# A mixture-of-experts stage: router weights applied on leaving PSUM, one-pass combine products, one-hot matrices built a pair ahead, and nine weight granules allowed ahead

## The chip, the core and the metric

The kernel runs on one core of a Trainium2 chip. The core has a matmul engine (PE, with its weight loads listed apart as PEld), a vector engine (DVE), a scalar engine (ACT), GpSimd (POOL) and a sync engine (SP), which here only issues DMAs. Matmul results land in PSUM, in eight banks of 128 x 512 float32; everything else lives in SBUF. The metric is the device time of one execution in microseconds (us), as the median of several runs. The profiled execution has its own time, and the rows shown are from it.

## The reference, cut to what matters

Two transformer-like blocks follow each other on 256 tokens of width 1024. The change touches the first block's mixture of experts alone: each token picks one of four groups and two of the eight experts in it, so 32 experts see on average 16 tokens each. All arithmetic is float32.

```python
def hier_moe(xn, w_gr, b_gr, w_er, b_er, w_gate, w_up, w_down):
    ...
    top_v, top_i = lax.top_k(e_logits, TOP_K_IN_GROUP)
    wts = g_prob[:, None] * jax.nn.softmax(top_v, axis=-1)
    ...
    def expert_block(args):
        tok_b, e = args
        xb = xpad[tok_b]
        h = jax.nn.silu(xb @ w_gate[e]) * (xb @ w_up[e])
        return h @ w_down[e]
    out = lax.map(expert_block, (buf_tok.reshape(n_blk, MOE_BLOCK), blk_expert))
    out = out.reshape(rows, d) * buf_wt[:, None].astype(out.dtype)
    y = jnp.zeros((t + 1, d), out.dtype).at[buf_tok].add(out)[:t]
```

## The kernel before, in words

The program goes through the first block's mixers (span 0 to about 130 us), the router (to about 148 us), the mixture of experts (148 to 625 us), the second block's attention (to about 810 us) and its table lookups (to the end). Every engine executes its instructions in the order in which the program issues them; waits are semaphores that the framework places by tile.

**Slots.** Each expert has 64 slots (a branch, `overflow`, serves inputs in which an expert gets more, and is passed over here). `Pp` holds, for each token and expert, the token's slot (1 to 64, or 0), `Wt` its router weight. For a group of four experts `Dm` (L749) is the 0/1 matrix tokens x slots, made on DVE by comparing `Pp` with a row of numbers. `gather(g)` (L747) multiplies the normalised tokens by it: 32 matmuls at L762, whose results leave PSUM through ACT and DVE into `xg`. `Dw` (L753) is the same matrix times `Wt`, made on POOL.

**Pairs.** The loop at L791 takes 16 pairs of experts; pair p uses group p // 2. For each pair PE does, in this order: the gate products (L807, two experts side by side in the array's columns), the combine of the pair before, the up products (L807 again), two transposes of `Dw` (L817), four of the hidden activations `hs` (L823), in an odd pair the gather of the next group, and the down products (L842). The combine (L775) multiplies `dT`, the transposed weighted matrix, by the experts' outputs `eo`: four float32 matmuls of 128 x 512, each of which the profile counts as two instructions; DVE adds each result to the residual `res` (L777). `dT`, `hT` and the two halves of `eo` leave PSUM by `evac` (L119), which alternates between ACT and DVE, so `dT` and the first half of `eo` go by ACT and `hT` and the second half of `eo` by DVE.

**Weight granules.** Each expert has three weight matrices of 128 x 4096 float32, 2 MiB each; one such load is called a granule here. A pair takes six, the stage 96 (numbered here 0 to 95), all issued by SP at L309 in the order of use. `pump` (L299) emits loads, `free` says that a granule was used. Until granule 45 the granules go around nine buffers, six of `ring` and three of `ring2` (L644); then, since `ring2` is closed before pair 8 (L793), around six. `pump` emits a load when no more than `cap` = 6 granules are emitted and not freed. On the chip a load starts when the last reader of its buffer's former granule is done.

**The end of the stage.** In pair 15 the combine is split: its first half stands among the last down products (L840), the second at the end (L847). Behind each of its four results DVE multiplies by the final gain (L784) and ACT takes two sums of squares (L144), which the next stage's scaling waits for. ACT also splits the first chunks of the next stage's weights there (L164).

Of the kernel before, what the change touches and what calls it, by code (L numbers as in the profile page):

```python
# [8 lines left out]
F32 = mybir.dt.float32  # L9
F32R = mybir.dt.float32r  # L10
# [21 lines left out]
NRING = 6  # L32
NRING2 = 3
# [31 lines left out]
def _body(tc, A, out, dbg):  # L65
    nc = tc.nc
# [10 lines left out]
    with ExitStack() as ctx:  # L77
# [219 lines left out]
        R2_END = n_pre + 5 * (NRING + NRING2)  # L297

        def pump():  # L299
            while st["emitted"] < len(src) and st["emitted"] < st["freed"] + st["cap"]:  # L300
                i = st["emitted"]
                if rg[1] is None and n_pre + NRING <= i < n_pre + NRING + NRING2:
                    break
                p = rg[1] if rg[1] is not None and n_pre <= i < R2_END and (i - n_pre) % (NRING + NRING2) >= NRING else rg[0]
                w = p.tile([128, 4096], F32, tag="w", name="w")
                n = src[i].shape[1]
                for o in range(0, n, 1024 if i == 0 else n):
                    v = slice(o, o + (1024 if i == 0 else n))
# [338 lines left out]
        if True:  # L647
# [70 lines left out]
            with pool("p2b", 2) as q, pool("p2c", 1) as q1:  # L718
# [5 lines left out]
                def weights():  # L724

                    gd = pq.tile([128, 2, 4], F32, name="gd")
                    nc.vector.tensor_tensor(gd, gl, gm[:, :, None].to_broadcast([128, 2, 4]), op=ALU.subtract)
                    ge = pq.tile([128, 2, 4], F32, name="ge")
                    nc.scalar.activation(ge, gd, AF.Exp)
                    pe = pq.tile([128, 2, 2], F32, name="pe")  # L730
                    nc.vector.tensor_tensor(pe, tv[:, :, 0:2], tv[:, :, 0:1].to_broadcast([128, 2, 2]), op=ALU.subtract)
                    nc.scalar.activation(pe, pe, AF.Exp)
                    preload(AF.Silu)
                    gs = pq.tile([128, 2], F32, name="gs")
                    nc.vector.tensor_reduce(gs, ge, axis=AX.X, op=ALU.add)
                    s2 = pq.tile([128, 2], F32, name="s2")
                    nc.vector.tensor_reduce(s2, pe, axis=AX.X, op=ALU.add)
                    nc.vector.tensor_tensor(s2, s2, gs, op=ALU.mult)
                    nc.vector.reciprocal(s2, s2)
                    nc.vector.tensor_tensor(pe, pe, s2[:, :, None].to_broadcast([128, 2, 2]), op=ALU.mult)  # L740
                    nc.vector.tensor_tensor(E2, E2, pe[:, :, :, None].to_broadcast([128, 2, 2, 32]), op=ALU.mult)
                    nc.vector.tensor_tensor(Wt, E2[:, :, 0], E2[:, :, 1], op=ALU.add)
                    mc = pq.tile([128, 1], F32, name="mc")
                    nc.vector.tensor_reduce(mc, b2[:, 0:32], axis=AX.X, op=ALU.max)
                    nc.vector.tensor_copy(most, mc)

                def gather(g):  # L747
                    Dm = q1.tile([128, 2, 4, 64], F32R, name="Dm")
                    nc.vector.tensor_tensor(Dm, Pp[:, :, 4 * g:4 * g + 4, None].to_broadcast([128, 2, 4, 64]), io64, op=ALU.is_equal)  # L749
                    if g == 0:  # L750
                        weights()
                    Dw = q1.tile([128, 2, 4, 64], F32, name="Dw")
                    nc.gpsimd.tensor_tensor(Dw, Dm.bitcast(F32), Wt[:, :, 4 * g:4 * g + 4, None].to_broadcast([128, 2, 4, 64]), op=ALU.mult)  # L753
                    xg = q.tile([128, 8, 4, 64], F32, name="xg")
                    for kk in range(4):
                        b = bank()
                        for j in range(2):
                            k = 2 * kk + j
                            i = 0
                            for tt in range(2):  # L760
                                for hl in range(2):
                                    nc.tensor.matmul(b[:, j * 256:(j + 1) * 256], xh[:, hl, tt, k * 128:(k + 1) * 128],  # L762
                                                     Dm[:, tt].rearrange("p e s -> p (e s)"), start=(i == 0), stop=(i == 3))
                                    i += 1
                        for j in range(2):
                            k = 2 * kk + j
                            evac(xg[:, k].rearrange("p e s -> p (e s)"), b[:, j * 256:(j + 1) * 256], gc[:, C_N2 + k:C_N2 + k + 1], eng="av"[kk % 2])
                    G[g] = (xg, Dw)

                def combine(pend, then=None, halves=(0, 1)):  # L770
                    dT, eo = pend
                    for half in halves:
                        for tt in range(2):
                            b = bank()
                            nc.tensor.matmul(b, dT[:, tt * 128:(tt + 1) * 128], eo[:, half * 512:(half + 1) * 512], start=True, stop=True)  # L775
                            rs = res[:, tt, half * 512:(half + 1) * 512]
                            nc.vector.tensor_tensor(rs, rs, b, op=ALU.add)  # L777
                            if then is not None:
                                then(tt, half)


                def both(tt, half):
# [2 lines left out]
                    quarter_sq(res, ss, hs, tt, half, "a")  # L785
                    quarter_sq(yy, ss2, hs, tt, half, "a")

                gather(0)
                pend = None
                pyx = ExitStack()  # L790
                for p in range(16):  # L791
# [6 lines left out]
                        yy = py.tile([128, 2, D], F32, name="yy")  # L798
                        ss2 = py.tile([128, 2, 2], F32, name="ss2")
                    g, pr = p // 2, p % 2  # L800
                    xg, Dw = G[g]
                    pg, pu = bank(), bank()
                    for dst in (pg, pu):
                        w = [get(), get()]
# [4 lines left out]
                        free(2)  # L809
                        if dst is pg and pend is not None:  # L810
                            combine(pend)
                    hs = q.tile([128, 512], F32, name="hs")
                    nc.scalar.activation(hs, pg, AF.Silu)
                    nc.vector.tensor_tensor(hs, hs, pu, op=ALU.mult)  # L814
                    b = bank()
                    for tt in range(2):
                        nc.tensor.transpose(b[:, tt * 128:(tt + 1) * 128],  # L817
                                            Dw[:, tt, 2 * pr:2 * pr + 2].rearrange("p e s -> p (e s)"), ident)
                    dT = q1.tile([128, T], F32, name="dT")
                    evac(dT, b[:, :T])  # L820
                    b = bank()
                    for f in range(4):
                        nc.tensor.transpose(b[:, f * 128:(f + 1) * 128], hs[:, f * 128:(f + 1) * 128], ident)  # L823
# [2 lines left out]
                    if pr == 1 and g < 7:  # L826
                        gather(g + 1)
                    w = [get(), get()]
                    eo = q1.tile([128, D], F32, name="eo")
                    bh = [bank(), bank()]  # L830
                    pend = (dT, eo)
                    for half in range(2):
# [5 lines left out]
                        for f in range(4):  # L838
                            if p == 15 and half and f == 2:
                                combine(pend, both, (0,))  # L840
                            for j in range(2):
                                nc.tensor.matmul(bh[half][64 * j:64 * j + 64, :], hT[:, f, 64 * j:64 * j + 64],  # L842
                                                 w[j][:, f * 1024 + half * 512:f * 1024 + half * 512 + 512],
                                                 start=(f == 0), stop=(f == 3))
                        evac(eo[:, half * 512:(half + 1) * 512], bh[half])
                    free(2)
                combine(pend, both, (1,))  # L847
            dump("h2", res)
# [613 lines left out]
```

## Time and profile before

| what | us |
|---|---|
| median of 3 runs (1549.41 to 1551.52) | 1549.61 |
| the profiled execution | 1549.71 |
| its span, first to last instruction | 1547.9 |
| PE busy over the span | 1330.8 (86%) |
| DVE busy | 774.8 (50%) |
| POOL busy | 399.4 (26%) |
| ACT busy | 383.9 (25%) |

The program moves 530 MB, 343 GB/s over the span. A span's average says little here: the stages have different limits, so the rows below are of the mixture of experts alone. "issue" in the chain of waits is time in which an engine waited for nothing that the profile shows. The granted clock is the share of the full TensorE clock that was granted in a stretch.

### The profile page before, as it was taken

The numbers are of one execution on the slowest core, as the hardware profiler recorded it, in microseconds if no ns is written. First come the engines' busy times: TensorE is split into PE (matmuls) and PEld (weight loads), VectorE is DVE, ScalarE is ACT, GpSimd is POOL, SyncE is SP. The second block draws the span as 40 slices with busy tenths as digits, with TensorE's granted clock in tenths as the row PEclk, the third lists the DMA queues.
The fourth block names the chain that finished last, engine by engine and source line by source line (L and its number), as shares of the span: only waits on it lengthen the run. The fifth ranks groups of instructions, "written<-read, shape, count | busy, mean of one in ns | idle before, by whom it ended". The sixth has DMA issues, their size and how long they took to land.

```text
span 1547.9 us, 16059 instructions
## 1 busy us (share of the span) xinstructions
PE 1330.8 (86%) x5543; PEld 712.6 (46%) x5543; DVE 774.8 (50%) x1796; ACT 383.9 (25%) x873; POOL 399.4 (26%) x355
## 2 busy tenths in 40 slices
PE   9899999999999999999999757877788777877777
PEld 7776334343344343788878723332333333332332
DVE  4756122122112121667577998877644544544453
ACT  6634000000000001546645322222111111111111
POOL 1211000000000000243111324444544445544441
PEclk9999999999999999999999878999998899999899
DMA  9526899996999999744330669999999999999994
GB/s 390 211 109 272 344 426 426 429 426 283 419 412 429 425 415 429 281 177 150 112 134 15 252 269 420 420 419 420 420 421 419 421 420 420 419 420 420 420 420 168
DMA packets 57748, 530.21 MB, mean 343 GB/s; under 512 B 6593, under 2 KB 6849, under 8 KB 9409
## 3 DMA queue, kind: packets, MB, share of 16 engines
q0 software_dynamic: 37936, 272.65, 42.8%
q1 hardware_dynamic: 19440, 256.35, 40.0%
q8 instruction: 46, 0.75, 0.2%
q14 instruction: 38, 0.30, 0.1%
q10 hardware_dynamic: 288, 0.16, 0.0%
HBM read 528.08 MB, written 1.05 MB: 342 GB/s over the span
## 4 chain that ended last, share of the span: by engine, by line
PE 27%; DMA 26%; DVE 8%; issue 8%; POOL 5%; ACT 1%; POOLq 0%; DVEq 0%; ACTq 0%
DMA rw<-in_uv_dram,ei 26%; PE b L807 7%; PE b L234 6%; POOL rw L1245 4%; PE b L842 4%; PE acc L1266 2%; DVE jk L1250 2%; PE b L775 2%; PE b L263 1%; PE b L247 1%; PE b L762 1%; DVE sl L165 1%; PE b L1014 1%; DVE i L1211 1%; DVE i L1216 0%
## 5 line engine op out<-in xcount | busy, mean ns | idle before, releaser
L1266 PE MATMUL acc<-rw,dg 128*128 128x512 f32 x1024 | 501.5, 648 | 148.6 <-ACT dg L1263 148.6
L1250 DVE SCALAR_TENSOR_TENSOR jk<-rw,xr 128x1024 f32<-128x1024 f32 x256 | 313.7, 1226 | 245.4 <-DMA rw<-in_uv_dram,ei 245.2
L1266 PEld LDWEIGHTS acc<-rw,dg 128*128 128x128 f32 x1024 | 206.9, 207 | 443.2 <-issue 233.3
L1245 POOL DMA_INDIRECT rw<-in_uv_dram,ei x256 | 301.6, 1178 | 390.5 <-PE acc L1266 283.8
L807 PE MATMUL b<-w,xg 128*64 128x512 f32 x1024 | 226.1, 594 | 1.6 <-DVEq L1315 1.6
L165 DVE TENSOR_TENSOR sl<-w,sh 128x512 fp32r<-128x512 f32 (+1 forms) x193 | 137.4, 719 | 81.4 <-ACT sh L164 80.7
L1263 ACT ACTIVATE dg<-kc,act 128x128 f32<-128x128 f32 x256 | 81.8, 390 | 283.3 <-DVE act L1260 283.3
L164 ACT ACTIVATE sh<-w 128x512 fp32r<-128x512 f32 (+1 forms) x200 | 120.7, 619 | 108.3 <-PE b L234 72.3
L807 PEld LDWEIGHTS b<-w,xg 128*64 128x64 f32 x1024 | 75.7, 137 | 146.8 <-issue 138.6
L842 PE MATMUL b<-w,hT 128*64 128x512 f32 x512 | 113.6, 595 | 7.4 <-issue 6.6
L234 PE MATMUL b<-nT,sh 128*128 128x256 f32 x576 | 108.3, 288 | 3.2 <-ACT sh L164 1.7
L753 POOL TENSOR_TENSOR Dw<-Dm,Wt 128x512 f32<-128x512 f32 x8 | 8.3, 1042 | 389.4 <-DVE Dm L749 383.7
L777 DVE TENSOR_TENSOR res<-res,b 128x512 f32<-128x512 f32 x64 | 44.0, 688 | 125.3 <-PE b L775 125.3
L234 PEld LDWEIGHTS b<-nT,sh 128*128 128x128 f32 x576 | 90.3, 193 | 9.4 <-issue 4.7
L234 PE MATMUL b<-nT,sl 128*128 128x256 f32 x288 | 82.5, 287 | 3.0 <-DVE sl L165 2.9
L842 PEld LDWEIGHTS b<-w,hT 128*64 128x64 f32 x512 | 38.6, 137 | 71.3 <-issue 69.3
L1255 ACT ACTIVATE act<-act 128x4 f32<-128x4 f32 x64 | 13.2, 205 | 225.3 <-DVE jk L1250 225.3
L814 DVE TENSOR_TENSOR hs<-hs,b 128x512 f32<-128x512 f32 x16 | 11.0, 687 | 109.6 <-PE b L807 109.6
L129 DVE COPY eo<-b 128x512 f32<-128x512 f32 x16 | 11.1, 691 | 101.1 <-PE b L842 101.1
L775 PE MATMUL b<-eo,dT 128*128 128x512 f32 x128 | 59.5, 606 | 1.2 <-DVE eo L129 1.2
L247 PE MATMUL b<-sh,nT 128*128 128x512 f32 (+1 forms) x192 | 58.3, 380 | 0.5 <-ACT sh L164 0.5
L234 PEld LDWEIGHTS b<-nT,sl 128*128 128x128 f32 x288 | 55.5, 193 | 4.1 <-DVE sl L165 4.1
(404 smaller groups left out, 1297.9 us busy)
## 6 DMA issues: line engine op xcount, KB each, us to landing
w<-in_w_gate_dram SPq DMA_DIRECT2D x32, 2048.0 KB, 14.5
w<-in_w_up_dram SPq DMA_DIRECT2D x32, 2048.0 KB, 14.4
w<-in_w_down_dram SPq DMA_DIRECT2D x32, 2048.0 KB, 13.6
w<-in_w_in_dram SPq DMA_DIRECT2D x13, 2048.0 KB, 14.5
w<-in_w_out_dram SPq DMA_DIRECT2D x4, 2048.0 KB, 13.2
w<-in_w_q_dram SPq DMA_DIRECT2D x4, 2048.0 KB, 8.1
rw<-in_uv_dram,ei POOLq DMA_INDIRECT x256, 17.5
w<-in_w_in_dram SPq DMA_DIRECT2D x4, 512.0 KB, 7.3
```

The costliest lines, as they stand in the source:

```text
L164: nc.scalar.activation(hi, src, AF.Copy)
L165: (eng or nc.vector).tensor_tensor(lo, src, hi.bitcast(F32), op=ALU.subtract)
L234: nc.tensor.matmul(dst, l[:, c * 128:(c + 1) * 128], x[:, r, k, :], start=(k == 0 and c % 2 == 0 and i == 0), stop=(k == nk - 1 and i == 2 ...
L247: nc.tensor.matmul(bs[tt][:, :n], x[:, l, k, tt * 128:(tt + 1) * 128], r[:, :n], start=(k == 0 and i == 0), stop=(k == 7 and i == 2))
L775: nc.tensor.matmul(b, dT[:, tt * 128:(tt + 1) * 128], eo[:, half * 512:(half + 1) * 512], start=True, stop=True)
L777: nc.vector.tensor_tensor(rs, rs, b, op=ALU.add)
L807: nc.tensor.matmul(dst[64 * j:64 * j + 64, :], xg[:, k, 2 * pr + j, :], w[j][:, k * 512:(k + 1) * 512], start=(k == 0), stop=(k == 7))
L842: nc.tensor.matmul(bh[half][64 * j:64 * j + 64, :], hT[:, f, 64 * j:64 * j + 64], w[j][:, f * 1024 + half * 512:f * 1024 + half * 512 + 51 ...
L1245: nc.gpsimd.indirect_dma_start(got[k], None, A["uv"], bass.IndirectOffsetOnAxis(ap=ei[tt][:, s:s + 1], axis=0))
L1250: nc.vector.scalar_tensor_tensor(junk, got[k][:, 0:D], 1.0, xr[:, tt], op0=ALU.mult, op1=ALU.mult, accum_out=act[tt][:, s:s + 1])
L1263: nc.scalar.activation(dg, ident, AF.Copy, scale=v[:, j:j + 1])
L1266: nc.tensor.matmul(acc[tt][hf], dg, rw[:, D + hf * 512:D + (hf + 1) * 512], start=False, stop=(s + j == 127), skip_group_check=True)
```

## The change

Four edits. (1) `Dw` becomes a matrix of one pair, compared on DVE and weighted on POOL at the pair's start; after its transposes DVE makes from the same PSUM bank `dT` as an exact 0/1 matrix (`not_equal`, L831 of the changed kernel) and a column `wc` of the slots' weights (a sum over tokens, L832). (2) The experts' outputs are multiplied by `wc` on leaving PSUM and split in two parts of float32r, a format that a matmul takes in one pass: ACT writes the high part (L858), DVE the rest (L859). The combine does two float32r products for each former float32 product, into the same bank (L777). (3) `Dm` of the next group is made at the start of the odd pair (`places`), not just ahead of the gather. (4) `pump` may emit nine granules ahead while nine buffers exist. `hs` has one buffer instead of two.

```diff
-            while st["emitted"] < len(src) and st["emitted"] < st["freed"] + st["cap"]:
+            while st["emitted"] < len(src) and st["emitted"] < st["freed"] + (NRING + NRING2 if rg[1] is not None and n_pre + NRING <= st["emitted"] < R2_END + NRING else st["cap"]):
...
+                def places(g):
+                    ahead[g] = Dm = q1.tile([128, 2, 4, 64], F32R, name="Dm")
+                    nc.vector.tensor_tensor(Dm, Pp[:, :, 4 * g:4 * g + 4, None].to_broadcast([128, 2, 4, 64]), io64, op=ALU.is_equal)
+
                 def gather(g):
-                    Dm = q1.tile([128, 2, 4, 64], F32R, name="Dm")
-                    nc.vector.tensor_tensor(Dm, Pp[:, :, 4 * g:4 * g + 4, None].to_broadcast([128, 2, 4, 64]), io64, op=ALU.is_equal)
-                    if g == 0:
-                        weights()
-                    Dw = q1.tile([128, 2, 4, 64], F32, name="Dw")
-                    nc.gpsimd.tensor_tensor(Dw, Dm.bitcast(F32), Wt[:, :, 4 * g:4 * g + 4, None].to_broadcast([128, 2, 4, 64]), op=ALU.mult)
+                    Dm = ahead.pop(g)
...
-                            nc.tensor.matmul(b, dT[:, tt * 128:(tt + 1) * 128], eo[:, half * 512:(half + 1) * 512], start=True, stop=True)
+                            for hl in range(2):
+                                nc.tensor.matmul(b, dT[:, tt * 128:(tt + 1) * 128], eo[:, hl, half * 512:(half + 1) * 512], start=(hl == 0), stop=(hl == 1))
...
+                    if pr == 1 and g < 7:
+                        places(g + 1)
+                    xg = G[g]
+                    Dw = q1.tile([128, 2, 2, 64], F32, name="Dw")
+                    nc.vector.tensor_tensor(Dw, Pp[:, :, 2 * p:2 * p + 2, None].to_broadcast([128, 2, 2, 64]), io64[:, :, 0:2], op=ALU.is_equal)
+                    nc.gpsimd.tensor_tensor(Dw, Dw, Wt[:, :, 2 * p:2 * p + 2, None].to_broadcast([128, 2, 2, 64]), op=ALU.mult)
...
-                    dT = q1.tile([128, T], F32, name="dT")
-                    evac(dT, b[:, :T])
+
+                    wc = G["w"][:, 0:1]
+                    dT = q1.tile([128, T], F32R, name="dT")
+                    nc.vector.tensor_scalar(dT, b[:, :T], 0.0, None, op0=ALU.not_equal)
+                    nc.vector.tensor_reduce(wc, b[:, :T], axis=AX.X, op=ALU.add)
...
-                    eo = q1.tile([128, D], F32, name="eo")
+                    eo = q1.tile([128, 2, D], F32R, name="eo")
...
-                        evac(eo[:, half * 512:(half + 1) * 512], bh[half])
+                        v = slice(half * 512, (half + 1) * 512)
+                        nc.scalar.activation(eo[:, 0, v], bh[half], AF.Copy, scale=wc)
+                        nc.vector.scalar_tensor_tensor(eo[:, 1, v], bh[half], wc, eo[:, 0, v].bitcast(F32), op0=ALU.mult, op1=ALU.subtract)
```

DVE in pairs 1 and 2 before: `hs` is the product with the up result, `Dm` (L749) stands just ahead of the gather's evacuations `xg`.

```order
L777 TENSOR_TENSOR res<-res,b 128x512 x4
L814 TENSOR_TENSOR hs<-hs,b 128x512
L129 COPY hT<-b 128x512
L749 TENSOR_TENSOR Dm<-Pp,kc 128x512
L131 TENSOR_SCALAR xg<-b,gc 128x256 x4
L129 COPY eo<-b 128x512
L777 TENSOR_TENSOR res<-res,b 128x512 x4
L814 TENSOR_TENSOR hs<-hs,b 128x512
L129 COPY hT<-b 128x512
L129 COPY eo<-b 128x512
```

DVE in the same two pairs of the changed kernel:

```order
L751 TENSOR_TENSOR Dm<-Pp,kc 128x512
L809 TENSOR_TENSOR Dw<-Pp,kc 128x256
L779 TENSOR_TENSOR res<-res,b 128x512 x4
L823 TENSOR_TENSOR hs<-hs,b 128x512
L831 TENSOR_SCALAR dT<-b 128x256
L832 TENSOR_REDUCE gs<-b 128x1
L129 COPY hT<-b 128x512
L131 TENSOR_SCALAR xg<-b,gc 128x256 x4
L859 SCALAR_TENSOR_TENSOR eo<-b,gs,eo 128x512 x2
L809 TENSOR_TENSOR Dw<-Pp,kc 128x256
L779 TENSOR_TENSOR res<-res,b 128x512 x4
L823 TENSOR_TENSOR hs<-hs,b 128x512
```

`Dm` moved to the head of the odd pair; two operations (L831, L832) now stand between `hs` and `hT`, which is on DVE in odd pairs only; both halves of `eo` end on DVE.

ACT at the end of pair 15 before: `hs` is the activation, `eo` the first half of the outputs, `sh` the next stage's weights, and L144 the sums of squares.

```order
L813 ACTIVATE hs<-b 128x512
L125 ACTIVATE dT<-b 128x256
L125 ACTIVATE eo<-b 128x512
L164 ACTIVATE sh<-w 128x512 x3
L144 ACTIVATE hs,ss<-res 128x512
```

ACT there in the changed kernel:

```order
L822 ACTIVATE hs<-b 128x512
L858 ACTIVATE eo<-b,gs 128x512
L164 ACTIVATE sh<-w 128x512 x3
L144 ACTIVATE hs,ss<-res 128x512
L144 ACTIVATE hs,ss_2753<-yy 128x512
L144 ACTIVATE hs,ss<-res 128x512
L144 ACTIVATE hs,ss_2753<-yy 128x512
L858 ACTIVATE eo<-b,gs 128x512
```

The second half of `eo`, on DVE before, now starts on ACT, behind four sums of squares.

On SP the loads of the stage stand in the same order in both kernels, and each waits for the last reader of the same former granule as before.

## Rows read from the trace of the kernel before

**Rows 1.** Windows; us, busy PE PEld DVE ACT POOL (count), PEclk, DMA share, GB/s:

```profile
169.00:366.00 197.00, 186.19 (x837) 75.01 (x837) 40.13 (x63) 15.68 (x32) 3.13 (x3) 0.99 1.01 427
366.00:394.00 28.00, 24.46 (x128) 11.08 (x126) 4.42 (x8) 2.66 (x6) 1.85 (x2) 1.00 0.56 217
394.00:611.00 217.00, 205.63 (x911) 83.29 (x907) 43.56 (x68) 16.66 (x34) 3.12 (x3) 0.98 1.00 422
```

**Rows 2.** Chain in order of time, pairs 10 to 12, end: start, us, what:

```profile
447.88 6.87 PE b L807 x32
454.75 3.63 PE b L775 x8
458.38 7.07 PE b L807 x32
...
467.77 7.09 PE b L842 x32
...
485.36 7.07 PE b L807 x32
...
495.39 4.07 PE b L762 x32
499.46 7.02 PE b L842 x32
506.48 6.87 PE b L807 x32
...
613.44 5.37 PE b L842 x24
```

**Rows 3.** Instructions and landing of L309, pair 15's down granules:

```profile
L309 SPq DMA_DIRECT2D w<-in_w_down_dram x2: 328/356/385, 593.5 to 594.0; - x2
...
DMA to landing us min/median/max: 12.1/14.4/16.6
```

**Rows 4.** Timeline around granules 9, 50 and 51, and 52 and 53:

```profile
153.80 13.95 PE L807 MATMUL b<-w,xg 128*64 128x512 f32 x64
...
160.91 0.33 SPq L309 DMA_DIRECT2D w<-in_w_up_dram  x1
...
354.85 17.47 SPq L309 DMA_DIRECT2D w<-in_w_up_dram  x2
...
386.05 0.80 SPq L309 DMA_DIRECT2D w<-in_w_down_dram  x2
```

**Rows 5.** Timeline, PE, float32r products of 128 x 512 after the stage:

```profile
634.37 0.39 PE L247 MATMUL b<-sl,nT 128*128 128x512 f32 x1
634.60 0.62 PE L247 MATMUL b<-sh,nT 128*128 128x512 f32 x2
635.06 0.39 PE L247 MATMUL b<-sl,nT 128*128 128x512 f32 x1
```

**Rows 6.** Waits of PE, 200 to 610 us: total, times, longest:

```profile
PE b L762 <- DVE Dm L749: 8.8, 6, 1.5
...
PE b L842 <- issue: 5.8, 7, 0.8
```

**Rows 7.** Groups by form, 200 to 610 us: busy us, mean ns, idle:

```profile
L131 DVE TENSOR_SCALAR xg<-b,gc 128x256 f32<-128x256 f32 x28 | 12.3, 480 | 28.1 <-PE b L762 28.1
...
L129 DVE COPY eo<-b 128x512 f32<-128x512 f32 x14 | 9.7, 692 | 93.9 <-PE b L842 93.9
...
L125 ACT ACTIVATE eo<-b 128x512 f32<-128x512 f32 x14 | 8.4, 597 | 63.4 <-PE b L842 36.8 <-issue 26.6
```

**Rows 8.** Windows over two gathers, columns as in rows 1:

```profile
256.20:260.30 4.10, 4.01 (x33) 3.91 (x34) 0.88 (x2) 1.67 (x4) 1.04 (x1) 1.00 1.04 440
314.80:320.20 5.40, 5.31 (x32) 5.34 (x32) 0.88 (x2) 1.51 (x4) 1.04 (x1) 0.68 1.00 422
```

**Rows 9.** Timeline, DVE and ACT, the end of pair 15:

```profile
623.02 0.68 DVE L129 COPY eo<-b 128x512 f32<-128x512 f32 x1
623.19 0.63 ACT L144 ACTIVATE hs<-yy 128x512 f32<-128x512 f32 x1 [0.21 <-DVE yy L784]
```

More of the change, by code (lines that the diff above doesn't have):

```diff
@@ L733, in weights @@
                     preload(AF.Silu)
-                    gs = pq.tile([128, 2], F32, name="gs")
+                    G["w"] = gs = pq.tile([128, 2], F32, name="gs")
                     nc.vector.tensor_reduce(gs, ge, axis=AX.X, op=ALU.add)
@@ L745, in weights @@
                     nc.vector.tensor_copy(most, mc)
+                ahead = {}
+                def places(g):
+                    ahead[g] = Dm = q1.tile([128, 2, 4, 64], F32R, name="Dm")
+                    nc.vector.tensor_tensor(Dm, Pp[:, :, 4 * g:4 * g + 4, None].to_broadcast([128, 2, 4, 64]), io64, op=ALU.is_equal)
                 def gather(g):
-                    Dm = q1.tile([128, 2, 4, 64], F32R, name="Dm")
-                    nc.vector.tensor_tensor(Dm, Pp[:, :, 4 * g:4 * g + 4, None].to_broadcast([128, 2, 4, 64]), io64, op=ALU.is_equal)
-                    if g == 0:
-                        weights()
-                    Dw = q1.tile([128, 2, 4, 64], F32, name="Dw")
-                    nc.gpsimd.tensor_tensor(Dw, Dm.bitcast(F32), Wt[:, :, 4 * g:4 * g + 4, None].to_broadcast([128, 2, 4, 64]), op=ALU.mult)
+                    Dm = ahead.pop(g)
                     xg = q.tile([128, 8, 4, 64], F32, name="xg")
@@ L767, in gather @@
                             evac(xg[:, k].rearrange("p e s -> p (e s)"), b[:, j * 256:(j + 1) * 256], gc[:, C_N2 + k:C_N2 + k + 1], eng="av"[kk % 2])
-                    G[g] = (xg, Dw)
+                    G[g] = xg
                 def combine(pend, then=None, halves=(0, 1)):
@@ L786, in both @@
                     quarter_sq(yy, ss2, hs, tt, half, "a")
+                places(0)
+                weights()
                 gather(0)
@@ L800, in _body @@
                     g, pr = p // 2, p % 2
-                    xg, Dw = G[g]
+                    if pr == 1 and g < 7:
[4 more added lines that the diff above has]
+                    nc.gpsimd.tensor_tensor(Dw, Dw, Wt[:, :, 2 * p:2 * p + 2, None].to_broadcast([128, 2, 2, 64]), op=ALU.mult)
                     pg, pu = bank(), bank()
@@ L811, in _body @@
                             combine(pend)
-                    hs = q.tile([128, 512], F32, name="hs")
+                    hs = q1.tile([128, 512], F32, name="hs")
                     nc.scalar.activation(hs, pg, AF.Silu)
@@ L817, in _body @@
                         nc.tensor.transpose(b[:, tt * 128:(tt + 1) * 128],
-                                            Dw[:, tt, 2 * pr:2 * pr + 2].rearrange("p e s -> p (e s)"), ident)
-                    dT = q1.tile([128, T], F32, name="dT")
-                    evac(dT, b[:, :T])
+                                            Dw[:, tt].rearrange("p e s -> p (e s)"), ident)
+                    wc = G["w"][:, 0:1]
+                    dT = q1.tile([128, T], F32R, name="dT")
+                    nc.vector.tensor_scalar(dT, b[:, :T], 0.0, None, op0=ALU.not_equal)
+                    nc.vector.tensor_reduce(wc, b[:, :T], axis=AX.X, op=ALU.add)
                     b = bank()
```

## The prediction

> **What bounds the kernel now.** I read first the windows by stage, then the chain of waits in order of time, then the sync engine's issues with their landings, then PE's waits. The windows show the stage running two engines at their limit together: from 169 to 366 us the DMA engines are busy for a share of 1.01 at 427 GB/s, and PE is busy for 186 of 197 us [rows 1]. The chain says which of the two ends last: it consists of PE alone, one block of products behind the other [rows 2], and PE's waits name `Dm` and short gaps, never a granule [rows 6]. From the start of pair 10 to the start of pair 12 PE takes 506.48 - 447.88 = 58.6 us, 29.3 a pair [rows 2]. Six granules of 2.097 MB at 427 GB/s take 6 x 4.91 = 29.5 us. So PE sets the end, but DMA has almost no speed to spare; what it has are pauses. Around pair 8 it moves 217 GB/s over 28 us, and behind it 422 over 217 us [rows 1]. At full rate those bytes need 28 x (1 - 217/427) = 13.8 us and 217 x (1 - 422/427) = 2.5 us less. The pause at pair 8 is the change from nine buffers to six: granule 51 takes the buffer of granule 45 and is issued at 372, 52 and 53 at 386, when the last products of pair 7 end [rows 4].
>
> **The combine.** Before, four float32 matmuls (eight instructions) take 3.63 us a pair [rows 2]. After, there are eight float32r products. Three such products of the same size stand 635.06 - 634.37 = 0.69 us apart, so one costs 0.23 [rows 5], and eight 1.84: 1.79 us saved in each of 15 pairs, and as much in the split combine of pair 15.
>
> **`Dm` a pair ahead.** PE waited for it 6 times in 200 to 610 us, 8.8 us in all, 1.47 each [rows 6]; the gathers are seven in the loop. The row before it in the queue at its new place is the former pair's `eo`, which is over by then; its 0.7 us lie beside gate products. The wait goes; next late would be `hT`, but the down products that need it stand behind a gather of at least 4.07 us [rows 2], so nothing takes its place in those pairs.
>
> **What is added.** On DVE a pair gets the comparison for `Dw`, `not_equal` and the sum over 128 x 256, and a subtraction for each half of `eo`, less a copy or two. For operations of this size the nearest rows are 0.48 us for 256 columns out of PSUM and 0.69 for 512 [rows 7]; some 2 us a pair, on an engine that is busy for 40 of 197 us [rows 1]. Neither the sum out of PSUM nor the comparison has a row of its own; the bounds are 0.2 and 0.69 us each. `dT` and the sum matter only where they precede `hT` on DVE without a gather behind: that is pair 15 alone (in even pairs `hT` is on ACT, of 0.60 us [rows 7]). There I take 2 x 0.48 = 1.0 us. `eo` needs two steps, 0.60 and 0.69, and has the whole gate block of 6.87 us before the combine reads it [rows 2, 7]; covered, except at the end. POOL's work is the same number of elements, half a pair earlier than needed.
>
> **Nine ahead.** Granule 9 is issued at 160.91, just as pair 0's gate products end (13.95 us of gate and up from 153.80, half of it is 160.8) [rows 4]. It waits for granule 0, nine before it: the loads run nine ahead already, since a load is held by its buffer and not by the place where the program emits it. I cost this edit at 0, between -1 and +1 us.
>
> **The sum.** PE needs (58.6 - 2 x 1.79 - 1.47) / 2 = 26.8 us a pair, DMA 29.5: from some pair on PE waits for granules, and the end is set by DMA. By pair 8 PE is earlier by 7 x 1.79 + 4 x 1.47 = 18.4 us. The buffers for 51 and for 52 and 53 come free at about 354 and 368 instead of 372 and 386, while DMA still works on granules issued before: the pause of 13.8 us goes. Of the 2.5 us of later gaps I take 2.0. At the end the last granule landed at 594.0 + 16.6 = 610.6 [rows 3] and was used from 613.44 [rows 2], a lead of 2.8 us which is used up; but PE itself is not ready at once: the up granules land 2 x 4.91 = 9.8 us earlier, and from there to the down products it takes 7.07 for the up products, 467.77 - 465.45 = 2.3 for the transposes [rows 2], and the 1.0 above, 10.4 in all, so 0.6 remain lost. That is 13.8 + 2.0 + 2.8 - 0.6 = 18.0 us. Behind it the second half of `eo` stands on ACT behind four sums of squares, the last of which begins at 623.19 and takes 0.63 plus a short read; then 0.60 and 0.69 follow, where a copy on DVE had ended at 623.70 [rows 7, 9]. That is some 1.5 us later, less 0.45 since the combine's first result comes sooner: +1.0 (0 to 2). The rest of the program hangs on this end and moves with it; its first granules stand right behind the last expert's in SP's queue, and land 4.9 us later than those, when the split on ACT asks for them. The profiled execution took 1549.71 us, 1.8 more than its span and 0.1 more than the median, so no correction: 1549.7 - 18.0 + 1.0 = 1532.7, and I say **1532.5 us**.
>
> **The skill's figure for the transfer.** No stretch of the trace shows more than 427 GB/s over 197 us [rows 1]. The Trainium skill, "DMA: Bandwidth & Descriptors", section "Where 436 GB/s comes from", puts the ceiling of the 16 ports at 435.2 GB/s. By that estimate the 182 MB between 169 and 611 us would take 8 us less than by the row, and the time would be about 1524; I keep the row.
>
> **Rivals.** (a) *The pause at pair 8 stays in part*, because PE is less early there than reckoned. For it: the clock. One gather took 5.31 us at a granted 0.68, that is partly at the lower of the two levels (1.2 of 2.4 GHz), where another took 4.01 at 1.00 [rows 8]; before each PE had waited for `Dm`. With PE waiting for granules such dips of 1.3 us may come more often. Against it: a PE that is slower waits less, so the loss ends where DMA takes over. Half of the 13.8 us gives 1540, all of it 1546.5. The Trainium skill, "TensorE: Matmul & The Clock Gate", section "HAM oscillation — how this bites in real kernels", says that a matmul loop which waits for DMA at every tile restarts at the low clock at every tile; by it, one dip in each of the last pairs leaves PE at 28.1 us a pair, still under DMA's 29.5, and the time about 1534. (b) *PE alone decides*, because DMA can go faster than it ever did: 16 x 1.79 + 7 x 1.47 = 38.9 us, less 1.0, gives 1512; against it stand the shares of 1.00 and 1.01 [rows 1]. (c) *Nothing is gained*, because DMA bounds the stage from its start and its pauses come from elsewhere: 1550; against it, PE never waits for a granule [rows 6]. (d) *Slower*: the float32r products with the exact 0/1 matrix cost as much each as a float32 matmul, 3.63 / 4 = 0.91 us. Then the combine takes 7.26 us, PE 29.3 + 3.63 - 0.74 = 32.2 us a pair, and 15 pairs add 43 us: 1593. It decides from (3.63 + 0.74) / 8 = 0.55 us a product; against it are the 0.23 of [rows 5].
>
> **How the numbers follow.** The forecast gets 0.62, with 1527 to 1538 as its own range (the last gaps and lead 3 us either way, the end 1, the added operations 1 or 2). Rival (a) gets 0.20, (b) together with a faster transfer 0.07, (c) 0.05, (d) with any other new stall of PE over 2.7 us a pair 0.06. The range of 1524 to 1543 holds the forecast, most of (a) and the edge of (b). About 0.2%, 3 us, can be told from no change. Faster: 0.62 + 0.20 + 0.07 = 0.89; the same 0.05; slower 0.06.
>
> **What will show it.** Right: the combine at about 1.8 us; PE waits for `w` from about pair 10 on, some 2 to 3 us a pair; DMA at 426 GB/s through pairs 7 and 8; the last down products start near 595. Wrong: no PE wait for granules in the later pairs, a DMA share below 0.95 around 366 to 394 us, products apart by 0.4 us or more, or granules that keep a lead of over 10 us to the end.

## The result, and the profile after

The changed kernel takes 1530.81 us (median of 4 runs, 1527.95 to 1532.5); the kernel before, measured beside it, 1550.56 (median of 4). The ratio is 0.9882, with a 95% interval of 0.986 to 0.9903: 19.75 us less. The forecast was 1532.5. A second measurement of the same changed kernel gave 1530.78 (1529.48 to 1535.34, ratio 0.9884 [0.9864, 0.9905]).

The profiled execution took 1527.95 us, with a span of 1526.2. First the windows over the experts' stage; the columns are those of [rows 1], and the last window is shorter since the stage ends earlier.

```profile
169.00:366.00 197.00, 189.04 (x924) 78.56 (x922) 53.80 (x97) 23.71 (x42) 5.41 (x9) 1.00 1.01 427
366.00:394.00 28.00, 25.73 (x114) 9.54 (x112) 6.24 (x11) 2.57 (x4) 0.34 (x1) 0.96 1.01 427
394.00:590.00 196.00, 182.49 (x834) 83.29 (x830) 47.12 (x86) 19.29 (x34) 4.32 (x7) 0.98 1.01 428
```

Look at the last column. Where [rows 1] had 217 GB/s from 366 to 394 us there are now 427, and 422 behind it has become 428: the pause of the transfers is gone, and so are the gaps. Before, DMA had pauses; now it has no free time in any of the three windows.

The chain of waits over pairs 11 and 12 of the changed kernel (start, us, what) answers to [rows 2]:

```profile
452.61 8.78 PE b L816 x30
461.39 2.05 PE b L777 x8
463.44 7.07 PE b L816 x32
...
472.00 3.83 PE b L763 x32
475.83 7.02 PE b L854 x32
482.84 6.87 PE b L816 x32
489.71 0.45 PE b L777 x2
490.16 21.14 DMA w<-in_w_gate_dram
```

In [rows 2] no transfer stood in this chain, only PE and, between its blocks, DVE's `hs` and `hT` of 0.7 us each. Now it ends in a transfer: the gate products of pair 13 wait for their granule, which lands at 511.3. From one such gate block to the other, 452.61 to 511.33, two pairs take 58.7 us, that is 29.4 a pair, which is the time of six granules (29.5) and no longer PE's. The combine (L777) takes 2.05 us for eight products.

PE's own waits from 200 to 590 us (total, times, longest), to set beside [rows 6]:

```profile
PE b L816 <- DMA w<-in_w_gate_dram: 8.2, 4, 2.4
PE b L835 <- DVE hs L823: 7.1, 14, 0.5
PE b L854 <- ACT hT L125: 4.8, 7, 0.7
PE b L816 <- SPq L1329: 2.3, 1, 2.3
```

The row with `Dm` is gone and granules have taken its place, in four gate blocks: 1.06 us at 393.47 and about 2.4 at 452.61, 511.33 and 570.25, which are pairs 9, 11, 13 and 15. The last row is no granule: one such stop at the start of pair 8 is in the kernel before (1.57 us) and in every kernel tried, also (2.3 us) in the one below whose gate products never wait for a transfer.

The end of the stage, PE, ACT and DVE in order of time (start, us, engine, line, operation, idle before):

```profile
589.46 1.04 PE L854 MATMUL b<-w,hT 128*64 128x512 f32 x2 [0.83 <-issue]
590.80 5.36 PE L854 MATMUL b<-w,hT 128*64 128x512 f32 x22 [0.29 <-DMA w<-in_w_down_dram]
...
600.82 0.67 ACT L858 ACTIVATE eo<-b,gs 128x512 fp32r<-128x512 f32 x1
601.52 0.75 DVE L859 SCALAR_TENSOR_TENSOR eo<-b,gs,eo 128x512 fp32r<-128x512 f32 x1 [1.43 <-ACT eo L858]
...
602.32 0.96 PE L777 MATMUL b<-eo,dT 128*128 128x512 f32 x3 [0.29 <-DVE eo L859]
...
602.86 0.69 DVE L779 TENSOR_TENSOR res<-res,b 128x512 f32<-128x512 f32 x1 [0.59 <-PE b L777]
...
603.13 6.39 PE L111 MATMUL b<-zero 128*128 128x512 f16 x21
...
608.12 1.34 ACT L158 ACTIVATE sc<-yy,r 128x512 f32<-128x512 f32 x2 [1.49 <-POOL r L878]
...
609.36 1.91 PE L185 MATMUL b<-kc,sc 128*128 128x128 f32 x16
```

PE begins the last down products at 589.46 with the granule that is there, and stops for the second, which lands at 590.8. Behind it the second half of `eo` goes through ACT and DVE, as the order of the two engines said it would.

The issue and landing of that last pair of granules, the counterpart of [rows 3]:

```profile
L309 SPq DMA_DIRECT2D w<-in_w_down_dram x2: 327/328/328, 567.1 to 567.6; - x2
...
DMA to landing us min/median/max: 19.0/21.1/23.2
```

567.6 + 23.2 = 590.8: the lead of 2.8 us that [rows 2, 3] showed has become zero. The forecast had these products start near 595; pair 0 began 4.0 us earlier here than in the kernel before (149.8 against 153.80).

### The profile page after: what moved, and what is told of

Same layout as the page of the kernel before. It is cut to its first block, busy times and chain, and to the rows that moved or that the text cites. A ratio compares the mean times of both kernels' runs of the same rounds, so it can differ in the third digit from the quotient of the medians.

```text
span 1526.2 us, 16072 instructions
## 1 busy us (share of the span) xinstructions
PE 1307.3 (86%) x5543; PEld 708.8 (46%) x5543; DVE 794.6 (52%) x1852; ACT 395.1 (26%) x881; POOL 406.5 (27%) x363
## 3 DMA queue, kind: packets, MB, share of 16 engines
HBM read 528.08 MB, written 1.05 MB: 347 GB/s over the span
## 4 chain that ended last, share of the span: by engine, by line
DMA 33%; PE 23%; issue 8%; DVE 6%; POOL 5%; ACT 1%; POOLq 0%; DVEq 0%; ACTq 0%
DMA rw<-in_uv_dram,ei 27%; PE b L234 6%; PE b L816 5%; POOL rw L1259 4%; DMA w<-in_w_gate_dram 4%; PE acc L1280 2%; PE b L854 2%; DMA w<-in_w_down_dram 2%; PE b L263 1%; DVE jk L1264 1%; PE b L247 1%; DVE sl L165 1%; PE b L763 1%; PE b L777 1%; PE b L111 1%
## 5 line engine op out<-in xcount | busy, mean ns | idle before, releaser
L1280 PE MATMUL acc<-rw,dg 128*128 128x512 f32 x1024 | 498.3, 644 | 151.6 <-ACT dg L1277 151.6
L1259 POOL DMA_INDIRECT rw<-in_uv_dram,ei x256 | 306.5, 1197 | 385.6 <-PE acc L1280 283.6
L816 PE MATMUL b<-w,xg 128*64 128x512 f32 x1024 | 238.5, 605 | 10.5 <-DMA w<-in_w_gate_dram 8.2
L816 PEld LDWEIGHTS b<-w,xg 128*64 128x64 f32 x1024 | 82.5, 139 | 155.0 <-issue 134.0
L810 POOL TENSOR_TENSOR Dw<-Dw,Wt 128x256 f32<-128x256 f32 x16 | 9.9, 618 | 389.7 <-DVE Dw L809 389.7
L779 DVE TENSOR_TENSOR res<-res,b 128x512 f32<-128x512 f32 x64 | 40.0, 683 | 100.9 <-PE b L777 100.9
L859 DVE SCALAR_TENSOR_TENSOR eo<-b,gs,eo 128x512 fp32r<-128x512 f32 x32 | 24.0, 751 | 114.7 <-ACT eo L858 112.0
L858 ACT ACTIVATE eo<-b,gs 128x512 fp32r<-128x512 f32 x32 | 22.0, 687 | 115.5 <-PE b L854 89.0
```

The costliest lines, as they stand in the source:

```text
L816: nc.tensor.matmul(dst[64 * j:64 * j + 64, :], xg[:, k, 2 * pr + j, :], w[j][:, k * 512:(k + 1) * 512], start=(k == 0), stop=(k == 7))
L859: nc.vector.scalar_tensor_tensor(eo[:, 1, v], bh[half], wc, eo[:, 0, v].bitcast(F32), op0=ALU.mult, op1=ALU.subtract)
L1259: nc.gpsimd.indirect_dma_start(got[k], None, A["uv"], bass.IndirectOffsetOnAxis(ap=ei[tt][:, s:s + 1], axis=0))
L1280: nc.tensor.matmul(acc[tt][hf], dg, rw[:, D + hf * 512:D + (hf + 1) * 512], start=False, stop=(s + j == 127), skip_group_check=True)
```

## The experiments

**The combine alone.** `Dm` stays where it was, just ahead of the gather, and six granules are allowed ahead.

```diff
...
-                    if pr == 1 and g < 7:
-                        places(g + 1)
...
                     evac(hT.rearrange("p f s -> p (f s)"), b)
                     if pr == 1 and g < 7:
+                        places(g + 1)
                         gather(g + 1)
```

> The one-pass combine (with the weights on leaving PSUM) without the rest: Dm is made again just ahead of the gather, and pump stops at six. My theory (PE gains until DMA bounds the stage): PE keeps its 7 waits of 1.47 us for Dm, so it needs (58.6 - 3.6) / 2 = 27.5 us a pair against DMA's 29.5; PE catches up with DMA later, but does, and nearly all of the gain stays: 1534 us (1531 to 1537), 3 us above the changed kernel. Rival, each part counts by its PE time: 16 x 1.79 = 28.6 us less than before, 1522. Rival, the Dm wait was what the pause at pair 8 hung on: no better than 1540.

Measured 1532.7 us (1530.83 to 1535.01), ratio 0.9891 [0.987, 0.9912]: 16.7 us less than before, against 19.75 for the whole change. PE's waits in its stage:

```profile
PE b L763 <- DVE Dm L751: 10.3, 7, 1.5
...
PE b L814 <- DMA w<-in_w_gate_dram: 2.4, 2, 2.0
```

All seven waits for `Dm` are there, 10.3 us, and cost little: where PE has them, it waits 2.4 us for granules instead of 8.2. In the later pairs either wait only fills the time up to the granule's landing. Around pair 8 a part of the pause stays (columns of [rows 1]):

```profile
366.00:394.00 28.00, 24.51 (x114) 9.25 (x112) 6.28 (x12) 2.57 (x4) 1.44 (x2) 1.00 0.94 388
```

At 388 instead of 427 GB/s that is 28 x (1 - 388/427) = 2.6 us, about the 3 us that were expected above the changed kernel. The medians are 1.9 us apart, less than these runs can tell.

**`Dm` alone.** The kernel before with the third edit only.

```diff
...
-                    Dm = q1.tile([128, 2, 4, 64], F32R, name="Dm")
+                    Dm = ahead.pop(g)
...
+                    if pr == 1 and g < 7:
+                        places(g + 1)
```

> The kernel before with Dm made at the start of the odd pair, nothing else. My theory: PE needs (58.6 - 1.47) / 2 = 28.6 us a pair, still less than DMA's 29.5, so its seven waits of 1.47 us come off in full, 10 us, since DMA's lead of about 20 us over PE is not used up: 1540 us (1538 to 1543). With e1's some 16 us the two parts alone sum to 26, 6 more than both together give: that difference is what DMA holds back. Rival, DMA already bounds the stage before: no gain, 1550. Rival, the change's gain is mostly the Dm wait: 1533 or less.

Measured 1535.46 us (1533.87 to 1538.07), ratio 0.9908 [0.989, 0.9927]: 14 us less and below the expected range, since seven waits of 1.47 us are 10.3. The windows of its stage (columns of [rows 1]):

```profile
169.00:366.00 197.00, 190.91 (x873) 76.36 (x870) 41.28 (x65) 16.09 (x33) 4.17 (x4) 1.00 1.01 428
366.00:394.00 28.00, 26.43 (x125) 11.22 (x126) 5.32 (x10) 2.88 (x6) 0.80 (x1) 1.00 0.83 338
394.00:597.00 203.00, 194.64 (x880) 77.36 (x876) 41.51 (x66) 16.48 (x34) 3.12 (x3) 1.00 1.01 428
```

The clock column tells where the rest comes from: 1.00 throughout, while [rows 1] have 0.99 and 0.98 and [rows 8] a gather at 0.68. In the kernel before, three of the seven gathers behind such waits (begun at 314.89, 435.32 and 553.99 us) ran partly at the lower level and took 5.5 to 5.6 us where the other four took 4.1, 1.5 us longer each (1.3 within the windows of [rows 8]); here all take 4.1. Seven waits and three dips are 10.3 + 4.4 = 14.7 us, and PE now waits 0.8 for a granule in pair 15. So a wait of 1.5 us cost up to 3.0. The middle window shows 338 GB/s: PE is not yet early enough here to remove the whole pause.

The two parts alone sum to 16.7 + 14.0 = 30.7 us and give 19.75 together. The other 11 do not come out, since DMA then sets the end.

**Six granules ahead.** The changed kernel without the fourth edit.

```diff
-            while st["emitted"] < len(src) and st["emitted"] < st["freed"] + (NRING + NRING2 if ... else st["cap"]):
+            while st["emitted"] < len(src) and st["emitted"] < st["freed"] + st["cap"]:
```

> The changed kernel with pump stopping at six granules again. My theory: loads are held by their buffers, not by pump; the sync engine's waits stay the same, and so does the time: 1531 us (1529 to 1533), with the ninth granule issued when pair 0's gate products end, as in both kernels. Rival, the nine ahead keep DMA busy through pair 8: without them its pause of some 13.8 us returns in whole or half, 1537 to 1545.

Measured 1532.91 us (1530.2 to 1534.64), ratio 0.9887 [0.9866, 0.9909]: not to be told from the changed kernel. The sync queue's issue of granule 9 (start, us, operation), here:

```profile
158.75 0.33 SPq L309 DMA_DIRECT2D w<-in_w_up_dram  x1
```

and in the changed kernel:

```profile
156.87 0.33 SPq L309 DMA_DIRECT2D w<-in_w_up_dram  x1
```

Pair 0 begins at 151.6 and at 149.8, so both issue it 7.1 us into the stage, when granule 0 has been read. The buffer holds the load, and not the place where it is emitted. The end of the stage is the same within the scatter too: from pair 0's first gate product to the next stage's first transposes it is 461.0 us here (151.64 to 612.62), 459.6 and 458.3 in two profiles of the changed kernel.

**Is it really DMA? Less work for PE.** The changed kernel without the combine of pairs 0 to 13.

```diff
-                        if dst is pg and pend is not None:
+                        if dst is pg and pend is not None and p == 15:
```

> The changed kernel with the combine of pairs 0 to 13 left out (the sums of those experts' outputs into the residual; pairs 14 and 15 are kept). PE loses 14 x 1.84 = 26 us more of work. My theory (DMA bounds the stage): the time stays, 1530 us (1526 to 1533), PE waits for granules some 4 to 5 us a pair, and the last granule lands within 2 us of where it did relative to granule 9. Rival, PE still decides: 1505. Rival, the longer waits drop the clock so often that it gets slower: above 1534, with the granted clock of the stage under 0.95.

One run: 1533.02 us, with 14 x 2.05 = 28.7 us of PE's work left out. PE's waits and the last window:

```profile
PE b L816 <- DMA w<-in_w_up_dram: 19.4, 9, 2.7
...
PE b L816 <- DMA w<-in_w_gate_dram: 11.6, 6, 2.7
```

```profile
394.00:593.00 199.00, 172.12 (x788) 70.13 (x784) 33.06 (x63) 19.94 (x35) 4.32 (x7) 0.97 1.01 428
```

The time left free on PE comes back as waits for granules, 31.0 us in 15 of them where the changed kernel has 8.2 in four, and the transfers run at 428 GB/s as before. The last granule lands 433.1 us after the issue of granule 9, in the changed kernel 433.9. The rival by which PE alone decides falls: it had this run at 1505.

**Is it really DMA? Fewer bytes.** The odd expert of a pair reads the down granule of the even one, so five granules a pair are loaded instead of six; the nine buffers serve the first 36 of 80 granules instead of 45 of 96.

```diff
...
-            src += [A[n][e + j] for n in ("w_gate", "w_up", "w_down") for j in range(2)]
+            src += [A[n][e + j] for n in ("w_gate", "w_up", "w_down") for j in range(2 if n != "w_down" else 1)]
...
-                    w = [get(), get()]
+                    w = [get()] * 2
...
```

> The changed kernel with five granules a pair: both experts of a pair use the first one's down granule, so half of the down weights are neither loaded nor used (the outputs of odd experts are left wrong by it). All instructions of PE, DVE, ACT and POOL stay. DMA then needs 5 x 4.91 = 24.6 us a pair, PE 26.8. My theory: PE decides again, never waits for a granule, and the part of the 38.9 us that DMA held back comes out: 12 to 14 us less than the changed kernel, 1517 us (1513 to 1521). Rival, PE's new stalls or its clock hold the stage, not the bytes: 1531.

Measured 1515.78 us (1512.61 to 1519.27), ratio 0.9788 [0.9762, 0.9814]. The windows of its stage:

```profile
169.00:366.00 197.00, 189.06 (x926) 78.45 (x923) 53.51 (x97) 23.68 (x42) 4.31 (x7) 1.00 0.90 366
...
394.00:557.00 163.00, 157.84 (x770) 64.88 (x767) 44.16 (x80) 18.66 (x33) 4.31 (x7) 1.00 0.96 393
```

DMA is at 366 and 393 GB/s, not at its limit; PE, busy for 189 of 197 and 158 of 163 us, never waits for a granule. This is what PE alone would give, 15 us below the changed kernel and 34 below the kernel before (1549.7 beside it). The 15 us are what the transfers hold back.

**The stage's last microseconds.** The last two granules are loaded by halves of their columns, the last `hT` goes to ACT, the 0.5 MB of the final gain is loaded behind the last granule, and the high part of the last half of `eo` goes to DVE, ahead of which no sums of squares stand; the cut shows this last edit.

```diff
...
-                        nc.scalar.activation(eo[:, 0, v], bh[half], AF.Copy, scale=wc)
+                        if p == 15 and half:
+                            nc.vector.tensor_scalar(eo[:, 0, v], bh[half], wc, None, op0=ALU.mult)
+                        else:
+                            nc.scalar.activation(eo[:, 0, v], bh[half], AF.Copy, scale=wc)
```

> The changed kernel with four small edits at the stage's end: both parts of the last half of eo on DVE, not behind the sums of squares on ACT; pair 15's hT on ACT; the last two granules loaded by column halves, so that the first half's products can begin 4.9 us earlier; and the 0.5 MB of the final gain loaded behind the last granule instead of at pair 8. My theory, the end hangs on the last landing: 1.2 us from the 0.5 MB, 1.3 from the halves (PE is ready 1.3 us before the last granule), 1 to 2 from the order on ACT and DVE: 1527.5 us (1525 to 1530). Rival, these lie beside other work: 1531.

Measured 1530.12 us (1528.88 to 1531.01), ratio 0.9879 [0.9859, 0.9899]. In its profile the way from the last down products to the next stage's first transposes is 17.7 us instead of 18.6; the medians (1530.12 and 1530.81) cannot be told apart. It was run again beside a second measurement of the changed kernel:

> The changed kernel as it is, on the same chip and in the same rounds as the next kernel, so that the two can be compared to less than 0.2%: 1531 us (1529 to 1533). In its trace: the time from pair 0's first gate product to the last down granule's landing within 1.5 us of the 441 us that the first trace of it shows, whatever the stages ahead of it take.

> The kernel with the four edits at the stage's end again, beside the changed kernel. My theory: from pair 0's first gate product to the next stage's first transposes it took 457.1 us against 459.6 in the first trace of the changed kernel, so it is 2 to 4 us faster: 1528 us where the changed kernel has 1531. Rival, that was the scatter of the two runs: no difference over 1 us.

The changed kernel gave 1530.78 and this one 1530.52 (1528.39 to 1531.28, ratio 0.9871 [0.9854, 0.9888]). In the new trace of the changed kernel the last granule lands 440.2 us after pair 0's first gate product, where 441 were expected within 1.5. From that product to the next stage's first transposes the profiles have 459.6 and 458.3 us without the edits and 457.1 and 455.9 with them, some 2.4 less each time; the medians have 0.7 and 0.3 less, and their ranges overlap. If the edits are worth anything, it is less than these runs can tell.

**Smaller granules.** If the buffers come free in halves, transfers could be asked for earlier. Each granule becomes two tiles with half of the columns; the edits of the stage's end are in it too. A half of gate or up is a contiguous 8 KB run in each partition, a half of down four runs of 2 KB.

```diff
...
+            for n in ("w_gate", "w_up"):
+                src += [halves(A[n][e + j])[h] for h in range(2) for j in range(2)]
+            src += [A["w_down"][e + j].rearrange("p (f c) -> p f c", f=4)[:, :, h * 512:(h + 1) * 512] for h in range(2) for j in range(2)]
...
```

> As e7, with every granule loaded as two halves of 1 MiB in buffers of their own (the same 18 MiB in all), each freed when its own products are done; the halves of a pair's two experts alternate. My theory: DMA's stream through the stage starts when the first buffer is free, and its length is fixed by the bytes, so a first buffer free after half of the gate products (3.5 us sooner) moves the whole stage's end by 3.5 us: 1524 us (1521 to 1527). Rival, halves are slower to move (more and smaller transfers, DMA under 420 GB/s): 1532 or above.

Measured 1545.15 us (1544.27 to 1547.64), ratio 0.9976 [0.9964, 0.9988]: nearly all of the gain is lost. The first window of its stage:

```profile
169.00:366.00 197.00, 190.71 (x926) 79.15 (x924) 52.58 (x95) 23.00 (x41) 4.30 (x7) 1.00 1.02 409
```

The share is 1.02 and the rate 409: the engines are as busy as before and move less. The release itself came as expected: the first half of granule 9 is issued 3.7 us into the stage (155.55 for a start at 151.87) instead of 7.1. To see whether it is the 2 KB runs, the down granules were then cut in whole rows, so that every half is an 8 KB run.

```diff
-            src += [A["w_down"][e + j].rearrange("p (f c) -> p f c", f=4)[:, :, h * 512:(h + 1) * 512] for h in range(2) for j in range(2)]
+            for n in ("w_gate", "w_up", "w_down"):
+                src += [halves(A[n][e + j])[h] for h in range(2) for j in range(2)]
```

> As the half granules before it, but the down granules are halved along their rows too, so that a half is one run of 8 KB in each partition (before it was four runs of 2 KB, and DMA moved 409 instead of 427 GB/s). My theory: the short runs cost the rate; with 8 KB runs the stream keeps 425 to 428 GB/s and the earlier first buffer shows: 1526 us (1523 to 1529). Rival, 8 KB runs, or twice as many transfers, are slower too: DMA at 409 to 415 GB/s and 1540 or above.

Measured 1533.49 us (1532.51 to 1534.79), ratio 0.9881 [0.9865, 0.9898], between the theory and its rival. The first window:

```profile
169.00:366.00 197.00, 189.23 (x926) 78.56 (x922) 53.37 (x96) 23.67 (x42) 4.30 (x7) 1.00 1.01 421
```

421 GB/s with every half one run of 8 KB, 427 with whole granules in runs of 16 KB. The 2 KB runs cost most of it, and the halves of 8 KB a little too. The DMA packets of the traces point to the runs, and not to the number of transfers by itself: between 200 and 360 us a packet of 16 KB takes 613 ns (median), one of 8 KB 312 and one of 2 KB 88, which is 26.7, 26.3 and 23.3 GB/s for each of the 16 engines. The table lookups of the changed kernel, other transfers in another queue, are in packets of 8 KB too: from 1000 to 1400 us these take 313 ns, at 420 GB/s. The earlier release does show here: the first half is issued at 155.27, 3.4 us earlier in the stage than in the changed kernel, but from there to the last landing it takes 439.5 us instead of 433.9. The lower rate takes back more than the release gave. So no kernel tried here with the whole work beats the changed one by more than can be told.

## Why the prediction was right, step by step

- **What bounds.** Right. The forecast's central claim was that the change speeds up PE and that DMA then sets the end. Taking 28.7 us from PE gained nothing (1533.02, one run), taking a sixth of the bytes gave 15 us (1515.78).
- **The combine.** Predicted 1.84 us, measured 2.05 in the chain. The size of a product was right: in the trace the eight begin 0.23 us apart, as in [rows 5], but 0.33 lies between the first two and 0.32 between the last and the up products. The 3.63 us of the kernel before contain such ends, the 1.84 did not, so a pair saves 1.58 us, not 1.79. The rival with products at 0.91 us falls with it.
- **The wait for `Dm`.** It went as said, and nothing took its place at the gathers. By itself it was worth more than the seven waits: the three dips of the clock that followed them went too. The rivals' paragraph had seen these dips in [rows 8], but the sum counted only the waits. That made no difference to the forecast, since DMA bounds.
- **The pause and the gaps.** Predicted 13.8 + 2.0 = 15.8 us. From the issue of granule 9 to the landing of the last, 160.91 to 610.6 took 449.7 us [rows 3, 4]; 156.87 to 590.8 takes 433.9. That is 15.8 less. That the two agree to the tenth is luck: 1 GB/s in the rates read is 1.0 us over the stage.
- **The lead.** Predicted 2.8 gained less 0.6, since PE was to be late for the last granule. The 2.8 are used up, and PE was there 1.3 us before it (589.46 against 590.8), so the 0.6 was not lost. From the first gate products to the held down products it was 613.44 - 153.80 = 459.6 us; now it is 590.80 - 149.8 = 441.0. The step gives 18.6, for 18.0 predicted.
- **The end of the stage.** Predicted +1.0; 17.5 us before (613.44 to 630.95) became 18.6 (590.80 to 609.36), +1.1. That these agree is partly luck. The rows of the kernel before that answer to those of the end above:

```profile
624.91 0.69 DVE L777 TENSOR_TENSOR res<-res,b 128x512 f32<-128x512 f32 x1 [1.22 <-PE b L775]
...
625.57 4.70 PE L111 MATMUL b<-zero 128*128 128x512 f16 x21
...
630.17 1.33 ACT L158 ACTIVATE sc<-yy,r 128x512 f32<-128x512 f32 x2 [1.49 <-POOL r L864]
...
630.95 1.97 PE L185 MATMUL b<-kc,sc 128*128 128x128 f32 x16 [0.68 <-ACT sc L158]
```

 Counted from the last down products, `eo` is over 1.2 us later (1.5 was reckoned), and the combine's first result, which DVE adds to `res`, comes 0.6 later (1.0 was reckoned). From there to the scaled input `sc` of the next stage both kernels take 5.26 us (624.91 to 630.17, 602.86 to 608.12). The other 0.5 had no term in the forecast: 21 PE products on zeros, which before took 4.70 us and ended ahead of `sc`, took 6.39 and ended behind it, at a granted clock of 0.59 and 0.51 from 603.2 to 607. In the second profile of the changed kernel they took 4.71, and PE waited 1.05 for `sc`.
- **Waits for granules.** Predicted "from about pair 10 on, some 2 to 3 us a pair". They come from pair 9 on, but at every second pair: 8.2 us in four, and 0.3 in the last down products. The windows show why (columns as above):

```profile
453.00:457.00 4.00, 4.00 (x14) 1.19 (x12) 0.00 (x0) 0.00 (x0) 0.09 (x1) 0.57 1.00 426
511.00:515.00 4.00, 3.67 (x10) 1.16 (x12) 0.08 (x1) 0.00 (x0) 0.62 (x1) 0.57 1.00 426
393.50:398.00 4.50, 4.50 (x22) 1.60 (x24) 0.53 (x2) 0.00 (x0) 0.62 (x1) 1.00 1.01 430
570.30:575.00 4.70, 4.70 (x22) 1.59 (x24) 0.00 (x0) 0.00 (x0) 0.00 (x0) 1.00 1.00 425
```

 Behind the waits at 452.61 and 511.33 the clock stood at 0.57, near the lower of its two levels (1.2 of 2.4 GHz), and the 30 gate products took 8.78 us, where at 570.25, at a clock of 1.00, they took 7.08. What PE needs when no granule is late can be read from the first pairs of the changed kernel, by their gate products:

```profile
201.21 7.04 PE L816 MATMUL b<-w,xg 128*64 128x512 f32 x32
...
226.46 7.04 PE L816 MATMUL b<-w,xg 128*64 128x512 f32 x32
...
254.80 7.04 PE L816 MATMUL b<-w,xg 128*64 128x512 f32 x32
```

 An even pair takes 25.3 us, an odd one, which has the gather, 28.3, and both 53.6: 26.8 a pair, as forecast. Against the 29.4 of the transfers most of the spare time thus falls behind the even pairs, which is where PE waits. Of the 58.7 - 53.6 = 5.1 us of two pairs a wait is 2.4 and the low clock 1.7; the rest stands around the wait, in the same block. Shorter delays lie elsewhere: three waits of the weight loads for up granules, 2.0 us in all. Rival (a) rested on such dips and saw that a slower PE waits less; so it was in these pairs, and the pause at pair 8 did not stay: 427 GB/s. The Trainium skill, "TensorE: Matmul & The Clock Gate", section "HAM oscillation — how this bites in real kernels", has a loop that waits for DMA at every tile start again at the low clock each time. Two of the four waits agree with it; those at 393.47 (1.06 us) and 570.25 (2.36 us) were followed by a clock of 1.00.
- **What is added on DVE and ACT.** Taken as covered, which holds: no row of PE's waits from 200 to 590 names one of the new operations. The one buffer of `hs` shows no cost either: PE waits at most 0.5 us for it, as before. The groups by form there (busy us, mean ns, idle):

```profile
L777 PE MATMUL b<-eo,dT 128*128 128x512 f32 x112 | 29.6, 406 | 0.0
L859 DVE SCALAR_TENSOR_TENSOR eo<-b,gs,eo 128x512 fp32r<-128x512 f32 x27 | 20.3, 751 | 96.0 <-ACT eo L858 93.3 <-ACTq L1329 2.7
L858 ACT ACTIVATE eo<-b,gs 128x512 fp32r<-128x512 f32 x27 | 18.6, 688 | 88.7 <-PE b L854 65.9 <-issue 22.8
...
L831 DVE TENSOR_SCALAR dT<-b 128x256 fp32r<-128x256 f32 x14 | 5.8, 418 | 0.0
L832 DVE TENSOR_REDUCE gs<-b 128x1 f32<-128x256 f32 x14 | 5.8, 415 | 0.0
```

 Between the bounds of 0.2 and 0.69 us that the forecast had, the comparison takes 0.418 and the sum 0.415 (0.48 was taken). The two parts of `eo` take 0.69 and 0.75, for 0.60 and 0.69. The 406 ns of L777 are how long one product is under way; one follows the other after 0.23.
- **Nine ahead.** Costed at 0. The changed kernel without it: 1532.91 against 1530.81, within what can be told.
- **The sum.** Predicted 18.0 - 1.0 = 17.0 us; in the two profiled executions 18.6 - 1.1 = 17.5. These two differ by 21.8 us: another 4.0 lie ahead of the stage (153.80 against 149.8 at its start), where the change touches nothing, and 0.3 behind it. In the second profile of the changed kernel the stage gives 18.9. Of the medians' difference of 19.75 that leaves 1 to 2 us outside the stage, less than the interval of the ratio, some 3 us either way. The windows ahead of it, in the kernel before:

```profile
60.00:152.00 92.00, 83.94 (x463) 65.27 (x462) 58.07 (x155) 43.80 (x80) 16.91 (x15) 0.94 0.46 183
```

 and in the changed kernel:

```profile
60.00:148.00 88.00, 79.25 (x461) 60.66 (x460) 57.57 (x154) 43.21 (x80) 15.89 (x14) 1.00 0.48 191
```

 The same work at a clock of 0.94 and 1.00, 4.7 us of PE's time apart. It is scatter between executions: the first gather begins 0.84 us behind the start of its `Dm` in both kernels (147.47 and 148.31, 144.93 and 145.77), and other kernels with the changed program up to there begin pair 0 as late as 153.7 us.

## What to carry to other kernels

Where two engines are both near their limit, reckon each one's time a stage by itself: a gain on the one ends where the other begins, and what parts bring alone (30.7 us here) is no sum of what they bring together (19.75). Ask of the second engine where its pauses are and what ended them; unless its stream can start earlier or carry less, they are all it has to give, and here their length, read from the rate of each window, was the forecast to within 1 us. Before moving a load earlier, look at which buffer it waits for: where that holds it, the place of its emission is worth nothing.

## What the runs showed of the hardware

- The transfers' rate went by the length of the runs in a partition even where all are long: 427 to 428 GB/s with 16 KB, 421 with 8 KB, and 409 with 8 KB and a third of the bytes in 2 KB runs, at a DMA share of 1.01 to 1.02 each. In this stage, which is bound by transfers, the 409 made the kernel 14 us slower than the changed one.
- A wait of PE of 1.5 us could draw the lower clock: of the seven gathers behind such waits three ran at it in part in the kernel before and two with the combine alone, and none where the wait was gone; a wait of 2.36 us could also pass without it.
- Two profiles of the changed kernel itself reach the first gate products at 149.8 and at 151.7 us: 2 us of scatter arise ahead of the stage, where the granted clock was 1.00 in the one and 0.98 in the other (0.94 in the kernel before). That is more than the medians show for the edits of the stage's end.
